# Four joints of the MLP in an encoder block on one core: a norm's scale, a load queue, two products and the last piece of tokens moved

## The chip, the cores and the metric

The program runs on one core of a Trainium2 chip. The core has five engines with an in-order queue each: TensorE (PE in the profile, its weight loads are PEld), VectorE (DVE), ScalarE (ACT), GpSimd (POOL) and SyncE (SP). They meet through semaphores. PE multiplies into PSUM, DVE and ACT read PSUM and work on SBUF, POOL works on SBUF alone, and DMA transfers are issued from the queues of SP, ACT and POOL. The metric is the device time of one execution in microseconds.

## The reference

One encoder layer on 1024 tokens of width 1024, all in float32. What is touched here is the MLP behind the attention and the last norm:

```python
        x = x + merged @ w_out[l]

        h2 = _rmsnorm(x, norm2_w[l])
        x = x + jnp.square(jax.nn.relu(h2 @ w_ff1[l])) @ w_ff2[l]

    return _rmsnorm(x, final_norm_w)
```

`_rmsnorm` divides each token by the root of its mean square and multiplies by a weight for each channel. The hidden width is 4096.

## The kernel before

Everything stands with channels on the 128 partitions and tokens on the free axis. `Y` is the residual, eight tiles of 128 x 1024. A float32 operand is split into a high part, rounded by ACT to the matmul's input type (`split`, line 170, `operand`, `prep`), and a low part, the difference, made by DVE. A product is then three passes: high times high, high times low, low times high.

**A visit** (class `Visit`, lines 1076 to 1123) multiplies a 2 x 2 grid of blocks with seven products instead of eight, after Winograd. `load` fetches two raw weight tiles from SP's queue into three `wraw` slots (line 1090), `blocks` makes four sums of weights (1096 to 1099), `prep` splits one of the seven (1107, 1108), `product` runs 3 x g matmuls of 512 columns into one of three PSUM banks (1119). Products 1, 6, 7 and 4 follow each other in one bank, 5 and 3 in another; a bank must have been read before the next product is added to it. `run` keeps `prep` three products ahead.

**First stage**, visits f0 to f15 (g = 4, 84 matmuls each): the first matrix of the MLP. The operands `XT` come from `Y` without the norm's factor, which is a number for each token. That factor, `r2`, is made by `norm2` (line 1207): four matmuls with ones over the sums of squares `xsq`, then `rsqrt` (lines 187 to 192, eight ACT steps and four DVE steps). `each1` runs it ahead of the second product of f0. f0 runs its products in the order `EARLY` = 1, 5, 2, 3, 6, 7, 4, the other visits in `USUAL` = 1, 2, 6, 5, 7, 3, 4. `ff1_done` copies products 1, 6, 7 and 5 to SBUF (1248), adds, and calls `act` (1242, 1243), which takes relu times `r2` and squares it. The results and their sums go to `d_u` in DRAM, from SP's and ACT's queues.

**Second stage**: the second matrix. Units 12 and 13 of the hidden width go through it without Winograd (`plain(NP2)`, lines 1399 to 1424): four operand pairs are loaded from `d_u` on SP's queue (1404), weights by `wtile` (146, 148, 150), and for each of eight output tiles `mm3` runs 24 matmuls (157) whose sum is added to `Y` (1415). Between them two steps of `u_prep` for each product begin the units of the visits behind: a unit is three tiles of 128 x 1024 and one of 128 x 512, loaded from `d_u` on SP's queue (1322, 1330) and split (1323, 1324, 1331, 1332). Then visits y0 to y14 follow `PLAN`: y0 has one unit (21 matmuls), y1 two, y2 three, y3 to y11 four, y12 three, y13 two, y14 one. Visit y3 is the first that needs unit 3; from there each visit to y11 needs a unit more. `each2` frees old units, makes sure of the needed one and takes one step of `u_prep` with each product. `ff2_done` adds each product to `Y` (1349). All big tiles come from one pool of `NUNIT` = 35 slots (`mem`).

**Last stage**: units 14 and 15 are multiplied plainly, in four pieces of 256 tokens (`PIECES`, lines 1460 to 1483). For each piece and each of eight output tiles, 12 matmuls (1470), a sum into `Y` (1472), a square (1474, 1477) and a sum of the squares on POOL or DVE (1478). `finish` then runs one matmul with ones (1451), `rsqrt`, eight scalings (1456) and eight stores from SP's queue (1458); its parts are taken between the next piece's tiles, and for the last piece behind it.

The order of instructions on each engine is made by a list scheduler from the source's order, the data and the free slots; the source's order is a priority.

The three places that set the joints:

```python
        if v.name == "f0" and i == v.order[1] and not state1[0]:
            state1[0] = True
            norm2()
...
                nc.sync.dma_start(b.ap[:, sl], d_u[j0 + f // 2, q, :, RT if q or f % 2 else LT])
            split(a, b, b.ap)
...
    rest = iter(())
    for t0, t1 in PIECES:
```

## Time and profile before

| | us |
|---|---|
| median of three runs | 1676.75 |
| the three runs | 1674.54 to 1679.56 |
| the profiled execution, its own time | 1680.28 |
| its span in the profile | 1678.6 |

| engine | busy us | share of the span |
|---|---|---|
| PE | 1609.9 | 96% |
| PEld | 1329.0 | 79% |
| DVE | 1206.8 | 72% |
| ACT | 806.4 | 48% |
| POOL | 222.8 | 13% |

The MLP with the last norm takes the span from about 1016 us to its end. A busy share is a mean over the stretch it is taken from; matmuls overlap in the pipeline, so that a row's busy time for PE is best checked against the count of matmuls times the distance from one to the next. A timeline row merges neighbouring instructions of one kind: its second number is the whole stretch, and in square brackets stand the idle time before it and what ended it. "Issue" rows of SP are the moments at which transfers are sent off, not their landing.

### The profile page before, as it was taken

What the parts mean: (1) busy time and instruction counts of PE and PEld (TensorE: products, weight loads), DVE (VectorE), ACT (ScalarE), POOL (GpSimd) and SP (SyncE); (2) the same over time, 40 slices, a digit from 0 to 9 for tenths busy, and PEclk for the clock granted to TensorE, in tenths of its full rate; (3) what the DMA queues carried; (4) which work ended last, traced back from release to release, by engine and by line L of the source; (5) the groups of instructions that cost most, each with busy time, mean ns of one, the idle gap of its engine ahead of it and who ended that gap; (6) DMA issues with size and microseconds to landing.
All of it is one profiled execution on the core that took longest, in us unless ns stands there. A gap on an engine that the chain in (4) does not pass through costs nothing.

```text
span 1678.6 us, 21771 instructions
## 1 busy us (share of the span) xinstructions
PE 1609.9 (96%) x8201; PEld 1329.0 (79%) x8201; DVE 1206.8 (72%) x1751; ACT 806.4 (48%) x1365; POOL 222.8 (13%) x247
## 2 busy tenths in 40 slices
PE   8899999999989889999999998999999998999997
PEld 3687788877768877888878886888888777888886
DVE  5987999931335668888887668767776478788766
ACT  5567431441335558878762345444444443444333
POOL 1212100000003446545300000000000000000012
PEclk9999999999989999999999999999999999999998
DMA  4135243472234252111074211444343543444213
GB/s 180 62 108 132 80 163 113 139 213 88 76 101 132 57 163 89 39 39 39 26 250 138 89 50 56 164 149 152 138 165 118 190 167 113 163 163 145 82 57 101
DMA packets 85657, 196.87 MB, mean 117 GB/s; under 512 B 20128, under 2 KB 35744, under 8 KB 85296
## 3 DMA queue, kind: packets, MB, share of 16 engines
q1 hardware_dynamic: 61376, 153.95, 27.4%
q10 hardware_dynamic: 23360, 38.02, 6.5%
q0 software_dynamic: 816, 3.51, 1.0%
q8 instruction: 65, 1.06, 0.3%
q14 instruction: 40, 0.33, 0.1%
HBM read 135.22 MB, written 60.23 MB: 116 GB/s over the span
## 4 chain that ended last, share of the span: by engine, by line
PE 77%; DVE 9%; DMA 6%; ACT 4%; POOL 2%; issue 2%; ACTq 0%; SPq 0%; DVEq 0%; POOLq 0%
PE ps_z L157 15%; PE ps_af L1119 10%; PE ps_ay L1119 8%; PE ps_w L157 5%; PE ps_cf L1119 5%; PE ps_p L157 5%; PE ps_s L849 5%; PE ps_cy L1119 4%; PE ps_pv L891 4%; PE ps_pt L872 3%; PE ps_df L1119 2%; PE ps_y L157 2%; DMA f<-d_vl 2%; PE ps_y L1470 2%; PE ps_dy L1119 2%
## 5 line engine op out<-in xcount | busy, mean ns | idle before, releaser
L157 PE MATMUL ps_z<-u,wi_h 128*128 128x512 f32 x1088 | 258.0, 392 | 11.8 <-POOL u L171 2.9
L157 PEld LDWEIGHTS ps_z<-u,wi_h 128*128 128x128 f32 x1088 | 202.2, 188 | 58.7 <-ACT u L170 4.5
L1119 PE MATMUL ps_af<-u,f_w 128*128 128x512 f32 x768 | 182.4, 390 | 4.3 <-ACT u L1248 4.3
L1119 PEld LDWEIGHTS ps_af<-u,f_w 128*128 128x128 f32 x768 | 144.1, 188 | 34.9 <-ACT u L1248 5.1
L1119 PE MATMUL ps_ay<-u,y_w 128*128 128x512 f32 x576 | 140.5, 393 | 2.4 <-ACT y_w L1107 1.2
L157 PE MATMUL ps_z<-u,wi_l 128*128 128x512 f32 x544 | 136.2, 401 | 0.0
L1119 PEld LDWEIGHTS ps_ay<-u,y_w 128*128 128x128 f32 x576 | 108.3, 189 | 27.1 <-ACT y_w L1107 2.4
L1478 POOL TENSOR_TENSOR u<-u,q 128x256 f32<-128x256 f32 x20 | 15.3, 767 | 822.2 <-ACT q L1477 821.9
L157 PEld LDWEIGHTS ps_z<-u,wi_l 128*128 128x128 f32 x544 | 104.4, 194 | 22.2
L849 PE MATMUL ps_s<-u,u 128*128 128x512 f32 x384 | 104.9, 406 | 2.0 <-POOL u L838 1.4
L150 DVE TENSOR_TENSOR wi_l<-wi_r,wi_h 128x1024 fp32r<-128x1024 f32 x34 | 41.5, 1220 | 77.0 <-PE ps_z L157 61.5
L1119 PE MATMUL ps_cf<-u,f_w 128*128 128x512 f32 x384 | 95.3, 398 | 0.0
L852 DVE TENSOR_REDUCE sx<-ps_s 128x1 f32<-128x1024 f32 x64 | 77.9, 1218 | 19.5 <-PE ps_s L849 17.5
L854 ACT ACTIVATE u<-ps_s,sx 128x1024 f32<-128x1024 f32 x64 | 72.3, 1130 | 31.8 <-DVE sx L852 31.4
L1119 PEld LDWEIGHTS ps_cf<-u,f_w 128*128 128x128 f32 x384 | 73.6, 192 | 16.3 <-issue 0.5
L878 DVE TENSOR_TENSOR u<-ps_pt,u 128x512 fp32r<-128x512 f32 x128 | 82.2, 679 | 5.1 <-ACT u L877 5.1
L148 ACT CAST wi_h<-wi_r 128x1024 fp32r<-128x1024 f32 x34 | 35.7, 1050 | 104.0 <-PE ps_z L157 95.6
L856 POOL TENSOR_SCALAR u<-u,sx 128x1024 f32<-128x1024 f32 x64 | 72.4, 1135 | 84.7 <-DVE sx L855 81.9
L849 PEld LDWEIGHTS ps_s<-u,u 128*128 128x128 f32 x384 | 67.5, 189 | 14.1 <-POOL u L838 2.2
L1108 DVE TENSOR_TENSOR f_w<-f_r,f_w 128x512 fp32r<-128x512 f32 x48 | 33.1, 690 | 58.4 <-ACT f_w L1107 58.4
L1243 ACT ACTIVATE u<-u 128x512 f32<-128x512 f32 x64 | 40.5, 633 | 71.1 <-DVE u L1242 70.2
L1119 PE MATMUL ps_cy<-u,y_w 128*128 128x512 f32 x288 | 71.3, 391 | 2.5 <-DVE y_w L1108 2.1
(376 smaller groups left out, 3307.3 us busy)
## 6 DMA issues: line engine op xcount, KB each, us to landing
u<-d_u SPq DMA_DIRECT2D x36, 512.0 KB, 3.6
wi_r<-w_in SPq DMA_DIRECT2D x34, 512.0 KB, 3.5
f_r<-w_ff SPq DMA_DIRECT2D x32, 512.0 KB, 3.2
d_u<-u SPq DMA_DIRECT2D x24, 512.0 KB, 4.0
d_z<-f ACTq DMA_DIRECT2D x20, 512.0 KB, 3.2
f<-d_z SPq DMA_DIRECT2D x20, 512.0 KB, 4.2
y_r<-w_ff SPq DMA_DIRECT2D x18, 512.0 KB, 3.8
d_u<-u ACTq DMA_DIRECT2D x16, 512.0 KB, 2.6
```

The source lines that it names most:

```text
L148: A.copy(hi, raw)
L150: V.tensor_tensor(lo, raw, hi.bitcast(F32), ALU.subtract)
L157: T.matmul(ps[:, sl], w, x[:, sl], start=start, stop=stop)
L849: T.matmul(pss[:, sl], a.r[:, qsl], b.r[:, sl], start=i == 0, stop=i == 2)
L852: V.tensor_reduce(sx[:, 0:1], pss, AX.X, ALU.max, negate=True)
L854: A.activation(P.ap, pss, AF.Exp, bias=sx[:, 0:1], accum_out=sx[:, 1:2])
L856: G.tensor_scalar(P.ap, P.ap, sx[:, 1:2], 1.0, ALU.mult, ALU.mult)
L872: T.transpose(pt[:, k * 128:(k + 1) * 128], P.ap[:, ko:ko + 128], ident)
L878: V.tensor_tensor(lv, p3, hf_, ALU.subtract)
L891: T.matmul(pso[:, 0:256], VC[kb].r[:, h * 128:(h + 1) * 128], PT[kg][i].r[:, k * 256:(k + 1) * 256], start=kb == 0 and i == 0, stop=kb == ...
L1119: T.matmul(ps, w[:, a, k * 128:(k + 1) * 128], self.xops[k][i].parts[b], start=n == 0 and i in FIRST, stop=n == 3 * self.g - 1, skip_group ...
L1243: A.activation(t, t, AF.Square)
```

## The change

- `norm2` is called ahead of the fifth product of f0 (product 6) instead of the second. Until it has been called, `act` keeps its work on a list (`waiting`), and the list is worked off right behind it; only product 2's block is on it by then.
- The loads of `u_prep` and of `plain` are issued from POOL's queue (`G`) instead of SP's.
- The plain products are a generator. Six of eight run ahead of the visits; the seventh is put ahead of y0's second product, the eighth ahead of y1's second. The last weight tile is loaded and split ahead of the visits, into a pair of `mem`, and the operands are freed behind the eighth product. `each2` starts a new unit only if seven slots of `mem` are free.
- The pieces are 320, 320, 256 and 128 tokens. For the last one, the squares of the eight tiles stand in one tile and are summed by eight matmuls with ones into one PSUM bank; the norm's weight is multiplied in ahead; the factor is made in 128-column steps, and two multiplications of 512 columns are stored with two transfers, one from SP's queue and one from ACT's.

```diff
@@ -43,7 +43,7 @@
 
 
 ORDER = "kkkmrvGGklGtvSvvGsciiSigiigcSSgiQigQQiiQgQgQigQgiQqgigoggiKVKVViKgigogigzzqggzqKqzggV"
-PIECES = tuple((i, i + 256) for i in range(0, S, 256))
+PIECES = ((0, 320), (320, 640), (640, 896), (896, 1024))
 K0 = 6
 LEAD, LAG = 3, 2
 VS, VS2 = (3, 4), (0, 1)
@@ -1231,16 +1231,21 @@
 
     d_u = dr.tile([NP1, 4, 128, 1024], F32, name="d_u")
 
+    scaled, waiting = [], []
+
+    def act(t, src, half_):
+        if not scaled:
+            waiting.append((t, src, half_))
+            return
+        V.scalar_tensor_tensor(t, src, 0.0, r2.ap[:, half_], ALU.max, ALU.mult)
+        A.activation(t, t, AF.Square)
+
     def ff1_done(j):
         sa, sb = mem.alloc(), mem.alloc()
         uu = [mem.alloc() for _ in range(4)]
         s = {1: sa.ap[:, LT], 6: sa.ap[:, RT], 7: sb.ap[:, LT], 5: sb.ap[:, RT]}
         (b11, b21), (t2, t1), (t3, b22), (t4, b12) = [(u.ap[:, LT], u.ap[:, RT]) for u in uu]
         seen, bank = set(), []
-
-        def act(t, src, half_):
-            V.scalar_tensor_tensor(t, src, 0.0, r2.ap[:, half_], ALU.max, ALU.mult)
-            A.activation(t, t, AF.Square)
 
         def done(i, ps):
             seen.add(i)
@@ -1278,12 +1283,12 @@
                 t.free()
         return done
 
-    state1 = [False]
-
     def each1(v, i):
-        if v.name == "f0" and i == v.order[1] and not state1[0]:
-            state1[0] = True
+        if v.name == "f0" and i == v.order[4]:
             norm2()
+            scaled.append(True)
+            for w in waiting:
+                act(*w)
 
     class Lazy:
         def __init__(self, make):
@@ -1319,7 +1324,7 @@
             if len(ii) == 2:
                 hi, lo = mem.alloc(True), mem.alloc(True)
                 units[j] += [hi, lo]
-                nc.sync.dma_start(lo.ap, d_u[j, q])
+                G.dma_start(lo.ap, d_u[j, q])
                 A.copy(hi.r, lo.ap)
                 V.tensor_tensor(lo.r, lo.ap, hi.ap, ALU.subtract)
                 for i, sl in zip(ii, HS):
@@ -1327,7 +1332,7 @@
             else:
                 t = mem.alloc(True)
                 units[j].append(t)
-                nc.sync.dma_start(t.ap[:, RT], d_u[j, q, :, LT])
+                G.dma_start(t.ap[:, RT], d_u[j, q, :, LT])
                 A.copy(t.r[:, LT], t.ap[:, RT])
                 V.tensor_tensor(t.r[:, RT], t.ap[:, RT], t.ap[:, LT], ALU.subtract)
                 UT[j][ii[0]] = Half(t.r[:, LT], t.r[:, RT])
@@ -1389,7 +1394,9 @@
                     for t in units[j]:
                         t.free()
             need(PLAN[q][0])
-        if not preps and nextj[0] < NP2 and nextj[0] - len(freed) < LIVE:
+        if q in (0, 1) and i == v.order[1]:
+            next(pp)
+        if not preps and nextj[0] < NP2 and nextj[0] - len(freed) < LIVE and mem.live + 7 <= NUNIT:
             preps.append(u_prep(nextj[0]))
             nextj[0] += 1
         if preps and next(preps[0], preps) is preps:
@@ -1401,27 +1408,38 @@
         for f in range(4):
             a, b = mem.pair()
             for q, sl in zip(((0, 3), (0, 2))[f % 2], HS):
-                nc.sync.dma_start(b.ap[:, sl], d_u[j0 + f // 2, q, :, RT if q or f % 2 else LT])
+                G.dma_start(b.ap[:, sl], d_u[j0 + f // 2, q, :, RT if q or f % 2 else LT])
             split(a, b, b.ap)
             ul.append((a, b))
         return ul
 
-    ul = plain(NP2)
-    for mp in range(4):
-        w = wtile(w_ff2t[0, mp], f"w2_{mp}")
-        for m in (2 * mp, 2 * mp + 1):
-            ps = pa(f"ps_y{m}")
-            mm3(ps, w, m % 2 * 4, ul)
-            V.tensor_tensor(Y[m], ps, Y[m], ALU.add)
-            for _ in range(2):
-                if not preps and nextj[0] < 3:
-                    preps.append(u_prep(nextj[0]))
-                    nextj[0] += 1
-                if preps and next(preps[0], preps) is preps:
-                    preps.pop()
-    for a, b in ul:
-        a.free()
-        b.free()
+    def plain_products():
+        ul = plain(NP2)
+        for mp in range(4):
+            if mp < 3:
+                w = wtile(w_ff2t[0, mp], f"w2_{mp}")
+            for m in (2 * mp, 2 * mp + 1):
+                ps = pa(f"ps_y{m}")
+                mm3(ps, w if mp < 3 else [x.r for x in w3], m % 2 * 4, ul)
+                V.tensor_tensor(Y[m], ps, Y[m], ALU.add)
+                if m == 7:
+                    for t in w3 + [x for p in ul for x in p]:
+                        t.free()
+                yield
+
+    pp = plain_products()
+    for m in range(6):
+        next(pp)
+        for _ in range(2):
+            if not preps and nextj[0] < 3:
+                preps.append(u_prep(nextj[0]))
+                nextj[0] += 1
+            if preps and next(preps[0], preps) is preps:
+                preps.pop()
+    raw = wp.tile([128, 1024], F32, tag="wraw", name="w2_3r", bufs=3)
+    nc.sync.dma_start(raw, w_ff2t[0, 3])
+    w3 = list(mem.pair())
+    split(*w3, raw)
 
     vs = []
     for q, (_, m, j0, j1) in enumerate(PLAN):
@@ -1457,19 +1475,21 @@
                                    ALU.mult, ALU.mult)
             nc.sync.dma_start(out[m * 128:(m + 1) * 128, sl], Y[m][:, sl])
 
+    def piece(sl, n, m):
+        wh, wl = w2[m // 2]
+        ps = pb(f"ps_y{m}_{sl.start}")
+        for j, (w, i) in enumerate(((wh, 0), (wh, 1), (wl, 0))):
+            for k in range(4):
+                o = ((m % 2) * 4 + k) * 128
+                T.matmul(ps[:, 0:n], w[:, o:o + 128], ul[k][i].r[:, sl], start=j + k == 0,
+                         stop=j == 2 and k == 3)
+        V.tensor_tensor(Y[m][:, sl], ps[:, 0:n], Y[m][:, sl], ALU.add)
+
     rest = iter(())
-    for t0, t1 in PIECES:
+    for t0, t1 in PIECES[:-1]:
         sl, n = slice(t0, t1), t1 - t0
         for m in range(8):
-            wh, wl = w2[m // 2]
-            ps = pb(f"ps_y{m}_{t0}")
-            for j, (w, i) in enumerate(((wh, 0), (wh, 1), (wl, 0))):
-                for k in range(4):
-                    o = ((m % 2) * 4 + k) * 128
-                    x = ul[k][i].r
-                    T.matmul(ps[:, 0:n], w[:, o:o + 128], x[:, sl], start=j + k == 0,
-                             stop=j == 2 and k == 3)
-            V.tensor_tensor(Y[m][:, sl], ps[:, 0:n], Y[m][:, sl], ALU.add)
+            piece(sl, n, m)
             if m == 0:
                 A.activation(xsq.ap[:, sl], Y[m][:, sl], AF.Square)
             else:
@@ -1479,9 +1499,39 @@
             if m > 1:
                 next(rest, None)
         rest = finish(sl, n)
+
+
+    t0, t1 = PIECES[-1]
+    sl, n = slice(t0, t1), t1 - t0
+    sq, yn, yo = (mem.alloc().ap.rearrange("p (m c) -> p m c", m=8) for _ in range(3))
+    psn = psA.tile([128, 512], F32, tag="A", name="ps_n4")
+
+    def square_sum(m):
+        T.matmul(psn[:, 0:n], ones, sq[:, m], start=m == 0, stop=m == 7)
+
+    for m in range(8):
+        piece(sl, n, m)
+        A.activation(sq[:, m], Y[m][:, sl], AF.Square)
+        A.activation(yn[:, m], Y[m][:, sl], AF.Copy, scale=pcol(NF + m))
+        if m > 0:
+            next(rest, None)
+        if m > 1:
+            square_sum(m - 2)
     for _ in rest:
         pass
-
+    square_sum(6)
+    square_sum(7)
+    r, a_, b_ = r3.ap[:, sl], half("m")[:, 0:n], half("t")[:, 0:n]
+    V.tensor_scalar(a_, psn[:, 0:n], 1.0 / D, eps_t[:, 0:1], ALU.mult, ALU.add)
+    A.activation(r, psn[:, 0:n], AF.Ln, bias=eps_t[:, 0:1], scale=1.0 / D)
+    A.activation(r, r, AF.Exp, scale=-0.5)
+    A.activation(b_, r, AF.Square)
+    V.scalar_tensor_tensor(b_, b_, -0.5, a_, ALU.mult, ALU.mult)
+    V.scalar_tensor_tensor(r, b_, 1.5, r, ALU.add, ALU.mult)
+    for m0, eng in ((0, nc.sync), (4, A)):
+        ms = slice(m0, m0 + 4)
+        V.tensor_tensor(yo[:, ms], yn[:, ms], bcm(r, 4), ALU.mult)
+        eng.dma_start(out.rearrange("(m p) s -> p m s", p=128)[:, ms, sl], yo[:, ms])
```

## Rows read from the trace of the kernel before

**Rows 1.** Stretch, length, busy PE PEld DVE ACT POOL (count), clock, DMA share, GB/s.

```profile
1015.60:1047.00 31.40, 27.14 (x103) 20.49 (x102) 27.00 (x43) 19.79 (x35) 0.00 (x0) 0.89 0.10 33
1047.00:1329.90 282.90, 282.90 (x1249) 233.94 (x1247) 193.79 (x306) 128.63 (x223) 0.00 (x0) 1.00 0.40 146
1329.90:1342.80 12.90, 8.72 (x30) 6.10 (x29) 6.92 (x7) 5.24 (x6) 0.00 (x0) 0.87 1.00 351
1342.80:1380.30 37.50, 37.50 (x165) 31.07 (x166) 26.74 (x32) 14.98 (x20) 0.00 (x0) 1.00 0.51 187
1380.30:1398.40 18.10, 13.26 (x45) 8.55 (x43) 16.99 (x29) 8.78 (x18) 0.00 (x0) 0.91 0.39 130
1398.40:1417.00 18.60, 18.57 (x82) 15.30 (x83) 17.04 (x31) 5.46 (x10) 0.00 (x0) 1.00 0.30 102
1417.00:1604.00 187.00, 187.00 (x826) 154.84 (x825) 145.62 (x217) 71.78 (x103) 0.00 (x0) 1.00 0.39 128
...
1614.90:1665.00 50.10, 49.88 (x400) 48.88 (x399) 35.69 (x76) 19.70 (x46) 15.11 (x20) 1.00 0.21 70
1665.00:1678.60 13.60, 1.23 (x3) 0.50 (x2) 6.11 (x15) 2.50 (x6) 0.23 (x1) 0.59 0.41 135
```

**Rows 2.** Chain that ended last: start us, us, engine, tile, line, count.

```profile
1316.34 2.72 PE ps_af L1119 x12
...
1645.89 11.50 PE ps_y L1470 x96
...
1657.40 0.45 PE ps_n L1451 x2
```

**Rows 3.** Instructions in order of time, joint 1: start, us, engine, line, operation.

```profile
1018.80 1.97 PE L1210 MATMUL ps_n<-f,ones 128*128 128x512 f32 x4
...
1020.61 0.67 ACT L187 ACTIVATE f<-ps_n,eps_t 128x512 f32<-128x512 f32 x1
...
1028.75 0.68 ACT L190 ACTIVATE m<-ps_n,eps_t 128x512 f32<-128x512 f32 x1
...
1029.83 0.59 ACT L1248 COPY u<-ps_af 128x512 f32<-128x512 f32 x1
...
1030.47 0.79 PE L1119 MATMUL ps_af<-u,f_w 128*128 128x512 f32 x1 [4.25 <-ACT u L1248]
...
1031.06 5.18 PE L1119 MATMUL ps_cf<-u,f_w 128*128 128x512 f32 x12
```

**Rows 4.** Waits of SP's queue, 1290 to 1345: us in total, times, longest.

```profile
SPq L146 <- DVE w_l L150: 4.5, 1, 4.5
```

**Rows 5.** Order of time, joint 2.

```profile
1326.34 1.75 SPq L1404 DMA_DIRECT2D u<-d_u  x4
...
1333.13 4.47 PE L157 MATMUL ps_y<-u,w_h 128*128 128x512 f32 x12 [3.19 <-ACT u L170]
```

**Rows 6.** Groups from 1380.3 to 1417: count | busy us, mean ns | idle before.

```profile
L1324 DVE TENSOR_TENSOR u<-u,u 128x1024 fp32r<-128x1024 f32 x5 | 6.1, 1219 | 1.1 <-ACT u L1323 1.1
...
L1107 ACT CAST y_w<-s 128x128 fp32r<-128x128 f32 x3 | 0.9, 300 | 1.3 <-PE ps_y L157 0.5 <-PE ps_ay L1119 0.4 <-PE ps_dy L1119 0.4
L1108 DVE TENSOR_TENSOR y_w<-s,y_w 128x128 fp32r<-128x128 f32 x3 | 0.8, 280 | 0.0
```

**Rows 7.** DMA issues: queue, count, KB each, median us to landing.

```profile
u<-d_u SPq DMA_DIRECT2D x36, 512.0 KB, 3.6
...
SY<-d_g POOLq DMA_DIRECT2D x2, 1024.0 KB, 10.1
```

**Rows 8.** Chain again, the tail.

```profile
1666.24 0.35 DVE f L1472
...
1667.60 1.24 PE ps_n L1451 x2
...
1673.28 1.58 DVE f L1456 x4
```

**Rows 9.** Line 467, one source line.

```profile
DMA to landing us min/median/max: 7.7/10.1/12.5
```

## The prediction

> **What bounds the kernel now.** I read the table of stretches first [rows 1], then the chain of work that ended last [rows 2], then each joint's order in time. In the long middles TensorE (PE) is never late: from 1047 to 1329.9 us, and again from 1417 to 1604, its busy time equals the stretch and the granted clock is 1.00. There a 512-column matmul costs 2.72/12 = 0.227 us, and a 256-column one 11.50/96 = 0.120 [rows 2]. So only the joints hold anything, and what each loses is its length less its matmuls at these prices.
>
> Joint 1, from 1015.6 to the end of the first MLP stage at 1329.9: 16 visits x 84 matmuls x 0.227 = 304.7, and 1.97 for the four norm matmuls [rows 3]. The first matmul starts at about 1015.9, so 314.1 are used and 7.4 lost. Joint 2 with the plain products, 1329.9 to 1380.3: 192 x 0.227 = 43.5 of 50.4, lost 6.9. Joint 3, visits y0 to y2, 1380.3 to 1417.0: 126 x 0.227 = 28.6 of 36.7, lost 8.1. All of that falls before 1398.4: 45 matmuls are worth 10.2 of 18.1 there, and 82 fill the next 18.6 [rows 1]. Joint 4, 1417 to 1665: 882 x 0.227 + 384 x 0.120 + three norms of 0.45 = 247.3 of 248, lost 0.7. Joint 5 is the tail behind PE's last product, 1665.0 to 1678.6: 13.6. Together 36.7 us are open.
>
> **The change part by part.**
>
> **Joint 1, scale later.** After product 1, PE runs norm2's four matmuls. ScalarE's (ACT's) in-order queue then takes norm2's eight steps between the casts for the last operands, the first at 1020.61 and the last at 1028.75. The two copies of line 1248, which free the banks for products 3 and 6, come only behind them, from 1029.83 on. PE stands idle for 4.25 us until they end, and the next 12 matmuls take some 5 us instead of 2.72 [rows 3]; the stretch's granted clock is 0.89 [rows 1]. Idle, slow matmuls and small change make the 7.4. The change moves norm2 three products later. From 1020.61 to the copy at 1029.83 ACT takes 17 instructions, 0.54 each, so the copies move up by about eight x 0.54 = 4.3 us, the whole idle, and with it goes the slow clock. What comes late next: the norm matmuls today cover the time in which the casts of XT[3] are made (1.97 less the 0.54 that these move up: 1.4), and after the move the eight steps stand before the copies of s[6] and s[7], which the last three products of f0 need one after the other on one bank. f1's first product also needs a bank that norm2's results hold. I charge 1.3 for the second and 1.4 for the first: 2.7 stay, 4.7 are gained. The bounds are 0, if the wait only moves, and 6.9. VectorE's (DVE's) one held-back scaling waits for r2; behind it stand other evictions of f0, which is part of the 1.3.
>
> **Joint 2, loads from POOL's queue.** SP's queue is in order. The second weight load of line 146 waits 4.5 us for a slot that a subtraction at line 150 frees [rows 4]. Behind it stand the eight loads of line 1404, the first four issued only at 1326.34, 3.6 us before PE is out of work, and PE's first plain matmul waits until 1333.13 for a cast of them [rows 5]. DMA share is 1.00 in that stretch [rows 1]: all comes at once. On POOL's queue the loads wait for their own slots alone. XT[..][1] and XT[..][2] are last read by the first two products of visit f15, so eight slots are free five products of 2.72 = 13.6 us before its end. POOL has nothing else to do: its busy time is 0.00 from 1015 to 1604 [rows 1]. Four casts on ACT and four subtractions of 1.22 on DVE [rows 6] then fall beside f15's last products; DVE is busy 194 of 283 us in that stage [rows 1]. I take 6.0 of the 6.9. The lower bound is 1, if the loads come as late as now and only the queue of issues is gone; the upper is 6.9.
>
> The Trainium skill, DMA: Bandwidth & Descriptors, section Issuing engines are not separate DMA queues, says that issuing from several engines only saves the issuing sequencer's time, since all run on the same 16 engines. By that rule joint 2 would give about 1 us instead of 6, a rival below. The rows on SP's waits speak against it here: what is saved is not issue time but a wait for someone else's slot in front.
>
> **Joint 3, two plain products in the first visits.** y0 and y1 have 1 and 2 blocks, so a product lasts 0.7 or 1.4 us, less than its cast, subtraction and eviction. DVE is busy 17.0 of 18.1 us [rows 1]. The two moved products are 48 x 0.227 = 10.9 us of PE work, with little DVE work (one sum of 1.2 us each). They leave the plain stage, so the visits begin 10.9 earlier, and fill a stretch that has 7.9 us of idle PE. Against it: six products instead of eight carry fewer steps of u_prep; unit 2 ends in y0, and the guard on free units keeps unit 3 waiting until the plain operands are freed in y1. Each unit is three subtractions of 1.22 [rows 6] and one of 0.68 = 4.3 us of DVE. From the plain stage to y3 DVE does 26.7 + 17.0 + 17.0 = 60.7 us [rows 1]; if the stretch shrinks from 74 to 68, that is 89%, and it is late-heavy. I let 3.1 of the 8.1 stay: 5.0 gained, bounds 1.5 (DVE bound throughout) and 7.5. Unit 3 is needed at y3, some 22 us after its slots come free, so its loads fit. The extra pair for the last weights is the same cast and subtraction, only earlier: nothing.
>
> **Joint 4** has nothing to give: 0, bounds -1 and +0.7. Behind POOL's last eight loads stand its additions of line 1478, which start only after them in data order anyway.
>
> **Joint 5, the tail.** The columns stay 1024, so the pieces cost the same by the line through 0.227 and 0.120 (0.066 at 128 columns). The 128-column price has no row; ends 0.066 and 0.120, I take 0.08, nearer the line: 96 x 0.014 = +1.3. Six sums of squares on PE ahead of the tail are worth 0.22 to 0.25 each: +1.4. PE so ends at about 1667.7. One more us for the last sum behind the third piece's eight scalings on DVE (now too it starts 1.2 behind PE, at 1666.24 [rows 8]): 1668.7. Then the chain, with 128-wide steps at 0.28 to 0.30 [rows 6] plus 0.06 between engines: addition and square 0.7, last sum 0.7 (1.24 now for 256 columns), three ACT steps 1.2, two DVE steps 0.7, two multiplications of 512 columns 1.4 = 4.7. Now the last scaling ends at 1674.86 [rows 8] and the span 3.7 us later; two stores of 256 KB on two queues instead of four waiting on one, some 3.0. The end is 1676.4: 2.2 gained. The bounds are 0 (128-column matmuls no cheaper than 256-column ones) and 5.
>
> **Sum**: 4.7 + 6.0 + 5.0 + 0 + 2.2 = 17.9. The profiled execution took 1680.28 for a span of 1678.6, so 1662.4 for it; it lies 3.5 above the median of the three runs, 1676.75. Against that median: 1658.9, say 1659.
>
> **The rivals.**
>
> *The queue buys nothing* (the rule above). If the loads wait for slots rather than for SP's order, joint 2 gives 1 and joint 3 half: 4.7 + 1 + 2.5 + 2.2 = 10.4, 1666. For it: SP's loads in the long stage do wait for slots. Against: the 4.5 us of [rows 4] directly ahead of the late loads.
>
> *The norm's wait comes back* (also the case that the change doesn't do what it says). The order on each engine is planned by data that is ready, not by the source alone: the norm matmuls may go into the same hole as now, or the copies of s[6] may wait as those of s[1] do. Joint 1 gives 0: 13.2, 1663.5.
>
> *Slower: POOL's loads land late.* Each visit of 84 matmuls is 19.0 us, and in it one unit's four loads must land, with 2.3 for the last cast and subtraction: the point is 4.2 us a load. SP's take 3.6, and POOL has only two large ones, of 1024 KB, issued together [rows 7]; the later took 12.5 [rows 9]. If loads of 512 KB took half of that later one each, 6.25, one after the other, a unit needs 25 + 2.3 = 27.3, and eight visits (y4 to y11) wait 8.2 each: +66 - 18, 1725. Against it: 2 MB in 12.5 us is 164 GB/s, so 512 KB in 3.2, and loads overlap.
>
> The Trainium skill, SBUF — State Buffer, section SBUF: two separate sides, adds that POOL's descriptors wait while VectorE runs a two-port mode, as a copy does. By that rule each load could wait for one DVE step, and joint 2 would lose 1 to 2 us; but DVE's steps in these stretches are two-source ones [rows 6], and no run here shows such a wait.
>
> *Every joint closes*: 6.9 + 6.9 + 7.5 + 5 = 26, 1650.
>
> **How the numbers follow.** Forecast 0.60, queue rival 0.14, norm rival 0.11, slower rival 0.06, all closed 0.09. A difference under 0.3% (5 us) can't be told from none. The queue rival's 10 us lie near that with its low ends: I put 0.05 of it, and 0.01 of the norm rival, at no change. Faster 0.60 + 0.09 + 0.10 + 0.09 = 0.88, same 0.06, slower 0.06. The range runs from 1650 (all closed) to 1669, where the queue rival has 3 us more to lose; beyond lie the slower case, the same and a few hundredths below.
>
> **What would show it.** Joint 1: copies of line 1248 ahead of the norm's ACT steps, and no PE gap over 2 us before f1. Joint 2: loads issued from POOL before 1320, and a plain matmul straight behind f15. Joint 3: PE idle in y0 and y1 under 4 us, DVE over 90%. Tail: some 11 us behind PE's last 128-column product. PE waits ahead of first products of y4 to y11 would show the slower case. Wrong would be the forecast if one of these waits stands again under another name.

## The result and the profile after

The changed kernel takes 1685.36 us (median of five runs, 1682.39 to 1689.15); the kernel before took 1677.23 beside it. The ratio is 1.0059, with a 95% interval of 1.0045 to 1.0073: slower by 0.6%, where 1659 had been forecast and 1650 to 1669 given as the range. The profiled execution after took 1685.28 us with a span of 1683.6, 5.0 more than the profiled one before.

The first step is to cut both spans at the same six points, so that every joint has a number. The points are read from PE's timeline: f0's first matmul, the end of f15, y3's first matmul (inside a merged row, by 0.227 us from one matmul to the next), y13's second product (its first row of `ps_dy`), the end of the last matmul of a piece, and the end of the span.

| stretch, us | before | after | difference | forecast |
|---|---|---|---|---|
| f0's first matmul to f15's end (joint 1) | 314.08 | 313.24 | -0.8 | -4.7 |
| f15's end to y3 (joints 2 and 3) | 87.03 | 86.88 | -0.2 | -11.0 |
| y3 to y13 (the long middle) | 187.05 | 189.75 | +2.7 | 0 |
| y13 to the end of the last piece | 61.00 | 68.47 | +7.5 | +3.7 |
| behind it | 13.59 | 8.43 | -5.2 | -5.9 |

With 1.0 of drift ahead of f0, where nothing was changed, these make the 5.0. The table of stretches of the changed kernel, which answers [rows 1] (stretch and length, busy PE, PEld, DVE, ACT, POOL with counts, clock, DMA share, GB/s):

```profile
1016.80:1047.00 30.20, 26.29 (x101) 20.11 (x100) 26.95 (x42) 20.27 (x35) 0.00 (x0) 0.89 0.10 35
...
1330.10:1341.60 11.50, 4.62 (x12) 3.31 (x12) 4.50 (x6) 5.35 (x6) 1.71 (x4) 0.76 1.03 410
1341.60:1373.90 32.30, 32.27 (x132) 26.51 (x133) 20.36 (x24) 8.69 (x12) 0.00 (x0) 0.93 0.09 31
1373.90:1398.00 24.10, 23.40 (x101) 18.44 (x100) 22.79 (x37) 12.05 (x21) 3.21 (x6) 1.00 0.48 153
1398.00:1417.00 19.00, 17.54 (x77) 13.90 (x76) 19.00 (x32) 7.37 (x12) 0.00 (x0) 1.00 0.35 112
1417.00:1606.70 189.70, 187.52 (x826) 154.68 (x825) 145.98 (x218) 69.96 (x103) 19.22 (x36) 1.00 0.37 127
...
1664.70:1675.10 10.40, 9.64 (x85) 9.46 (x84) 5.14 (x16) 5.42 (x18) 0.00 (x0) 1.00 0.32 102
```

Two lines speak at once. In the first one the clock is 0.89, as before: joint 1's hole is still there. And from 1330.1 to 1341.6 PE works 4.6 of 11.5 us while the DMA engines are full (share 1.03, 410 GB/s); in the next stretch they are nearly empty (0.09). Something was fetched too early and all at once.

**Joint 1** in the timeline after (start, us, engine, line, operation; in brackets the idle time before and what ended it), beside [rows 3]:

```profile
1020.92 1.88 PE L1210 MATMUL ps_n<-f,ones 128*128 128x512 f32 x4
...
1024.52 0.67 ACT L187 ACTIVATE f<-ps_n,eps_t 128x512 f32<-128x512 f32 x1
...
1028.24 0.63 ACT L188 ACTIVATE f<-f 128x512 f32<-128x512 f32 x1
...
1029.66 0.62 ACT L1136 CAST u<-t 128x512 fp32r<-128x512 f32 x1 [0.79 <-DVE t L1166]
...
1030.19 0.58 ACT L1253 COPY u<-ps_af 128x512 f32<-128x512 f32 x1
...
1030.82 0.79 PE L1119 MATMUL ps_af<-u,f_w 128*128 128x512 f32 x1 [3.91 <-ACT u L1253]
...
1031.41 4.98 PE L1119 MATMUL ps_cf<-u,f_w 128*128 128x512 f32 x12
```

The norm's matmuls stand in the old hole although the source calls them three products later, and four of its eight ACT steps (line 187 and 188, twice each) still run ahead of the copies. Counted from f0's first matmul the copy starts after 13.36 us, before after 13.98. It now stands behind a cast (line 1136) that itself waits 0.79 us for DVE. The hole is 3.91 us instead of 4.25, and the slow 12 matmuls are still 4.98.

**Joint 2** in the timeline after, beside [rows 5]:

```profile
1313.19 4.37 POOL L1411 DMA_DIRECT2D u<-d_u  x8 [484.46 <-DMA d_u<-u]
...
1330.83 0.63 ACT L1241 ACTIVATE u<-u 128x512 f32<-128x512 f32 x1 [1.36 <-DVE u L1240]
1330.93 0.54 POOL L1327 DMA_DIRECT2D u<-d_u  x1 [0.18 <-issue]
1331.37 1.03 ACT L170 CAST u<-u 128x1024 fp32r<-128x1024 f32 x1
...
1331.96 0.38 SPq L1090 DMA_DIRECT2D y_r<-w_ff  x1
...
1332.30 2.93 ACT L170 CAST u<-u 128x1024 fp32r<-128x1024 f32 x3
...
1332.45 4.62 PE L157 MATMUL ps_y<-u,w_h 128*128 128x512 f32 x12 [2.38 <-ACT u L170]
...
1340.15 0.29 DVE L1096 TENSOR_TENSOR s<-y_r 128x128 f32<-128x128 f32 x1 [6.50 <-DMA y_r<-w_ff]
1340.36 3.49 DVE L171 TENSOR_TENSOR u<-u,u 128x1024 fp32r<-128x1024 f32 x3
...
1341.63 1.65 PE L157 MATMUL ps_y<-u,w_h 128*128 128x512 f32 x3 [4.56 <-DVE u L171]
```

POOL sends the eight loads off at 1313, 13 us earlier than SP did, just as forecast. It is of little use, because the first cast (line 170) keeps its place on ACT behind the last step of f15 (line 1241). And POOL doesn't stop: behind these eight it has sent off thirteen unit loads (lines 1327 and 1335) by 1331.5. SP's load of `y_r`, 128 KB for y0, comes at 1331.96 into full DMA engines:

```profile
DMA to landing us min/median/max: 8.2/8.2/8.2
```

(one source line, 1090, in this stretch). Before, the same load took 5.2:

```profile
DMA to landing us min/median/max: 5.2/5.2/5.2
```

DVE's next instruction in order is line 1096, which needs `y_r`. It waits 6.50 us, and the three subtractions of line 171 that PE needs stand behind it, though the casts that they need are done by 1335.2. Over the whole execution, the units' loads of 512 KB take longer on POOL's queue than the 3.6 us of SP's [rows 7] (DMA issues after: queue, count, KB each, median us to landing):

```profile
u<-d_u POOLq DMA_DIRECT2D x36, 512.0 KB, 4.3
```

### The profile page after: what moved, and what is told of

It reads as the page before. It is cut to its first block, busy times and chain, and to the rows that moved or that the text cites. A ratio compares the mean times of both kernels' runs of the same rounds, so it can differ in the third digit from the quotient of the medians.

```text
span 1683.6 us, 21810 instructions
## 1 busy us (share of the span) xinstructions
PE 1616.2 (96%) x8215; PEld 1337.2 (79%) x8215; DVE 1206.4 (72%) x1744; ACT 806.7 (48%) x1372; POOL 256.0 (15%) x306
## 4 chain that ended last, share of the span: by engine, by line
PE 77%; DVE 8%; DMA 6%; ACT 4%; issue 3%; POOL 1%; SPq 0%; ACTq 0%; DVEq 0%; POOLq 0%
PE ps_z L157 17%; PE ps_af L1119 10%; PE ps_ay L1119 6%; PE ps_w L157 5%; PE ps_p L157 5%; PE ps_cf L1119 5%; PE ps_s L849 5%; PE ps_pv L891 3%; PE ps_cy L1119 3%; PE ps_pt L872 3%; PE ps_y L157 3%; PE ps_df L1119 2%; PE ps_y L1484 2%; DMA u<-d_u 2%; DMA f<-d_vl 2%
## 5 line engine op out<-in xcount | busy, mean ns | idle before, releaser
L1411 POOL DMA_DIRECT2D u<-d_u x16 | 8.6, 549 | 500.8 <-DMA d_u<-u 484.5
```

## The experiments

All but e12 are timed in five rounds against the kernel before on the same chip (median 1676.5 to 1676.9). The table gives the ratio with its interval, and the five stretches of the profiled execution. The first two rows repeat the result.

| run | ratio, 95% interval | f0 to f15's end | to y3 | to y13 | to the last piece's end | behind |
|---|---|---|---|---|---|---|
| before | 1 | 314.08 | 87.03 | 187.05 | 61.00 | 13.59 |
| after | 1.0059 (1.0045 to 1.0073) | 313.24 | 86.88 | 189.75 | 68.47 | 8.43 |
| e1_norm | 0.9997 (0.9985 to 1.0009) | 312.84 | 85.59 | 187.36 | 60.70 | 13.46 |
| e2_pool | 1.0041 (1.0028 to 1.0055) | 314.30 | 89.67 | 189.18 | 60.89 | 13.13 |
| e3_visits | 0.9993 (0.9981 to 1.0006) | 314.07 | 84.85 | 187.03 | 60.85 | 13.12 |
| e4_tail | 1.0051 (1.0036 to 1.0066) | 313.46 | 86.80 | 186.99 | 69.93 | 8.71 |
| e5_order | 0.9979 (0.9964 to 0.9995) | 308.46 | 86.48 | 187.60 | 60.60 | 13.47 |
| e6_plain | 0.9988 (0.9974 to 1.0002) | 314.14 | 83.06 | 187.89 | 60.89 | 13.87 |
| e7_units | 1.0049 (1.0034 to 1.0065) | 314.02 | 95.74 | 187.00 | 60.59 | 13.13 |
| e8_t256 | 1.0007 (0.9990 to 1.0023) | 314.42 | 86.48 | 187.00 | 62.57 | 11.39 |
| e9_three | 0.9943 (0.9927 to 0.9959) | 308.36 | 80.77 | 187.56 | 60.97 | 13.49 |
| e10_t384 | 0.9936 (0.9924 to 0.9948) | 308.37 | 80.85 | 187.38 | 62.26 | 11.31 |
| e11_sp_units | 1.0026 (1.0015 to 1.0037) | 313.88 | 80.99 | 187.95 | 75.58 | 8.74 |
| e12_tail_again | a single time, 1686.31 us | 313.45 | 86.98 | 187.00 | 74.52 | 8.73 |

Where a run leaves a stretch alone, it repeats within 1.0 us of the others (the one to y3 within 1.5), so the stretches can tell more than the totals, which spread by several us from run to run. The first four runs do one part of the change each.

### e1_norm: the scale later, alone

The edit is the hunks on `act`, `waiting` and `each1` of the change, and no other.

> The kernel before with the first part alone: the norm's scale taken three products later. Theory (after the trace of the changed kernel): the planner puts the norm's matmuls and ACT steps back into the same hole, so only 0.8 us are gained: ratio 0.9995, and PE again waits some 4 us for a copy of ACT ahead of the last products of f0. Rival (the forecast's term): 4.7 us gained, ratio 0.9972, and no PE gap over 2 us there.

Measured: 0.9997, and joint 1 is 1.2 us shorter, hardly more than the 1.0 by which that stretch repeats. The gap ahead of the copy's reader is 3.91 us again, ended by line 1253. The theory holds; the forecast's 4.7 don't come.

### e5_order: the copies planned ahead of the norm

```diff
+    def behind(ins):
+        for c in first:
+            tc.add_manual_dep(ins.ins, c.ins.name, nosync, reason="order")
...
-            A.copy(t.r[:, LT], src)
+            behind(A.copy(t.r[:, LT], src))
...
-        before = ln_exp_table(after) if after is not None else lambda ins: None
+        before = ln_exp_table(after) if after is not None else order
...
+        if v.name == "f0" and i == v.order[2]:
+            for _ in xo3:
+                pass
...
-                A.copy(s[i], ps)
+                ins = A.copy(s[i], ps)
+                if len(first) < 2:
+                    first.append(ins)
```

(`xo3` is the rest of `x_odd(3)`, the operands of products 7 and 4; `order` is `behind` for the norm's first step of each half. The dependency is for the plan alone and sets no semaphore.)

> The first part alone, and beside it an order laid down for the plan: the last three casts of operand XT[3] wait for nothing new, but the casts for products 7 and 4 and all eight ACT steps of the norm are planned behind the first two copies of f0. Theory: the copies' place in ACT's in-order queue is the cause of PE's gap; it falls from 3.9 us to under 1, the 12 matmuls behind it take 2.7 to 3 us instead of 4.6, f0's first matmul to f1's third product takes 25 us instead of 30: ratio 0.997. Rival: another wait takes its place (the operands for products 7 and 4, or r2): ratio 0.999 or above.

Its timeline, to be held against the one of joint 1 above:

```profile
1025.69 0.58 ACT L1259 COPY u<-ps_af 128x512 f32<-128x512 f32 x1
1026.17 0.59 ACT L1259 COPY u<-ps_cf 128x512 f32<-128x512 f32 x1
...
1026.33 0.96 PE L1119 MATMUL ps_af<-u,f_w 128*128 128x512 f32 x3 [0.84 <-ACT u L1259]
1027.12 2.91 PE L1119 MATMUL ps_cf<-u,f_w 128*128 128x512 f32 x12
```

The copy starts 10.30 us after f0's first matmul (1015.39) instead of 13.98, the gap is 0.84, and the 12 matmuls behind it take 2.91 instead of 5.18: the granted clock is 1.00 throughout. From f0's first matmul to f1's second product in its order (the first row of `ps_df` behind f0, which the theory calls the third) go 25.4 us, as the theory had it, against 31.0 before. The stretch is 5.6 us shorter than before, and the ratio 0.9979. Here is all that joint 1 promised, and the cause of its hole is shown: the copies' place in ACT's queue, not the call's place in the source. The edit takes two things from in front of the copies, the norm's steps and the casts for products 7 and 4; no run parts them.

### e2_pool, e6_plain, e7_units: which loads do the harm

Each puts loads from `d_u` on POOL's queue: e6 those of `plain`, e7 those of `u_prep`, e2 both.

```diff
-                nc.sync.dma_start(b.ap[:, sl], d_u[j0 + f // 2, q, :, RT if q or f % 2 else LT])
+                G.dma_start(b.ap[:, sl], d_u[j0 + f // 2, q, :, RT if q or f % 2 else LT])
...
-                nc.sync.dma_start(lo.ap, d_u[j, q])
+                G.dma_start(lo.ap, d_u[j, q])
...
```

> The kernel before with the second part alone: all loads from d_u (those of the plain operands and those of the units) issued by POOL. Theory: POOL puts more transfers on the DMA engines at once, SP's 128 KB load of y_r lands late, DVE's queue stands behind it, and one late unit load stalls DVE in the long middle: 4 us lost at the plain products, 2.7 more in the middle, together +6 to +7, ratio 1.004. Rival one (the forecast's term): 6.0 gained, ratio 0.9964. Rival two (the loads' order doesn't matter, the loss of the changed kernel came with its other parts): ratio within 0.001 of 1.

> The kernel before with only the eight loads of the plain operands on POOL's queue; the units' loads stay on SP's. Theory: the harm of the second part came from the units' loads, which nothing paces on POOL; without them y_r lands in some 4 us, PE's waits at the plain products are one of 2.4 us (ACT's first cast behind f15's last step), and joint 2 loses 3.5 to 4.5 instead of 6.9: ratio 0.998. Rival: early plain loads are of no use since the casts keep their place on ACT and DVE, ratio 0.9995 to 1.0005; or they do harm themselves: 1.002.

> The kernel before with only the units' loads on POOL's queue; the plain operands' stay on SP's. Theory: the units' loads fill the DMA engines ahead of the plain operands and of y_r; joint 2 loses 4 us or more over before, and the long middle 2 to 3 more: ratio 1.0035 to 1.005. Rival: only both together do harm: ratio within 0.001 of 1.

Together (e2) they lose: 1.0041, 2.6 us up to y3 and 2.1 in the middle. The plain loads alone (e6) gain 4.0 us up to y3 in the profile; the interval of the timed ratio, 0.9974 to 1.0002, holds these 4.0 and also none. The units' loads alone (e7) lose 8.7 there. PE's waits at the plain products, in e6:

```profile
1327.18 0.38 SPq L1090 DMA_DIRECT2D y_r<-w_ff  x1
...
1327.67 7.55 PE L157 MATMUL ps_y<-u,w_h 128*128 128x512 f32 x25 [2.38 <-ACT u L170]
...
1330.09 0.30 DVE L1096 TENSOR_TENSOR s<-y_r 128x128 f32<-128x128 f32 x1 [1.22 <-DMA y_r<-w_ff]
1330.30 3.49 DVE L171 TENSOR_TENSOR u<-u,u 128x1024 fp32r<-128x1024 f32 x3
```

and in e7:

```profile
1333.74 1.04 ACT L170 CAST u<-u 128x1024 fp32r<-128x1024 f32 x1 [6.31 <-DMA u<-d_u]
...
1334.84 5.20 PE L157 MATMUL ps_y<-u,w_h 128*128 128x512 f32 x12 [8.80 <-ACT u L170]
...
1341.53 0.29 DVE L1096 TENSOR_TENSOR s<-y_r 128x128 f32<-128x128 f32 x1 [5.48 <-DMA y_r<-w_ff]
```

In e6 SP sends `y_r` off ahead of the units' loads, it lands in 2.9 us, and DVE loses 1.22. What is left at the plain products is the wait of 2.38 and the low clock behind it (0.54 from 1328 to 1330; 25 matmuls in 7.55 us that are worth 5.7). In e7 fourteen unit loads have been sent by 1327.5; the first plain loads, which PE needs first, go off at 1322.4 behind eight of them, and `y_r` at 1328.7 behind all:

```profile
DMA to landing us min/median/max: 8.8/10.7/13.7
...
DMA to landing us min/median/max: 12.8/12.8/12.8
```

(lines 1404, eight plain loads, and 1090, `y_r`, of e7). So five runs give `y_r` 2.9 us without POOL's unit loads (e6), 5.2 before, 8.2 after and in e2, 12.8 in e7: the harm is the units' loads, which SP's order had held back behind the weights and the plain operands, and which on POOL wait for nothing but a free slot.

The Trainium skill, DMA: Bandwidth & Descriptors, section Issuing engines are not separate DMA queues, says that transfers from all issuing engines run on the same 16 engines and interleave, and that a second issuer only saves the sequencer's time. The first half is what e7 shows, at 8.7 us; the second half misses what decided here, since the queue also set the order in which the transfers were let go. By that rule joint 2 would have gained about 1 us. In e6 the plain products lose 4.0 us instead of 6.6, which is 2.6.

The 2.1 us in the middle of e2, and most of the 2.7 after, are one or two late transfers in front of an in-order engine. The chain of waits after:

```profile
1527.34 6.48 DMA u<-d_u
...
1533.84 1.06 ACT u L1328
...
1534.92 1.23 DVE u L1329
...
1537.48 0.61 DVE f L1354
...
1538.22 2.98 PE ps_ay L1119 x12
```

PE waits 1.4 us there for DVE's line 1354, which stands behind a unit's subtraction. Another 0.7 are lost at 1569, in a visit where DVE waits 2.1 us for a `y_r`; e11, whose units come from SP, has that wait too (0.7). In e2 it is a `y_r` that DVE waits 4.3 us for, and PE 1.6; in e7 PE doesn't wait in the middle at all, though its units come from POOL too. Why these loads are late in two of three such kernels stays open.

### e3_visits: two plain products in the first visits, alone

The edit is the hunks on `plain_products`, `pp` and the guard with `mem.live`, with all loads on SP's queue.

> The kernel before with the third part alone: two plain products moved into y0 and y1, all loads still on SP's queue. Theory: PE loses 3.7 us instead of 8.1 in y0 to y2, so 4.4 gained, ratio 0.9974. Rival: with SP's in-order queue the units' loads come late for y3 and give the gain back, ratio 0.999 to 1.001.

Measured: 0.9993, and 2.2 us less up to y3, half of the theory's 4.4. The rival is nearer. The engines' busy time in two stretches of e3 (columns as in the first table):

```profile
1369.00:1391.90 22.90, 21.83 (x95) 17.25 (x94) 20.10 (x34) 10.60 (x20) 0.00 (x0) 1.00 0.54 184
1391.90:1406.90 15.00, 12.73 (x51) 10.13 (x52) 15.00 (x25) 5.97 (x10) 0.00 (x0) 0.91 0.37 122
```

and what PE does in the second one:

```profile
1404.52 3.82 PE L1119 MATMUL ps_ay<-u,y_w 128*128 128x512 f32 x9 [2.27 <-DVE f L1349]
```

DVE is busy 15.00 of 15.00 us, some 6 of them with subtractions for units that came late; PE waits 2.27 for an eviction behind them, and then runs 9 matmuls in 3.66 us instead of 2.04. In e9 below, where the plain loads come early, the same wait of 2.25 us stays in y2, but the 9 matmuls behind it take 2.34 in their row and not 3.82. From y0 to y3 PE loses 6.2 us in e3, where the first unit load goes off 5.4 us behind f15's end, 4.6 in e9 and e11 (2.4 behind it), and 3.6 after (12.5 ahead of it). By these runs this part gives more where the units' loads are sent earlier.

### e4_tail, e12_tail_again, e8_t256: the tail alone

e4 and e12 are the kernel before with the change's `PIECES`, `piece` and new end. e8 changes one size in it:

```diff
-PIECES = ((0, 320), (320, 640), (640, 896), (896, 1024))
+PIECES = tuple((i, i + 256) for i in range(0, S, 256))
...
-    sq, yn, yo = (mem.alloc().ap.rearrange("p (m c) -> p m c", m=8) for _ in range(3))
+    sq, yn, yo = ([mem.alloc().ap.rearrange("p (m c) -> p m c", m=4) for _ in range(2)]
+                  for _ in range(3))
```

> The kernel before with the last part alone: pieces of 320, 320, 256 and 128 columns and the last piece's own end. Theory: a 128-column matmul takes 0.108 us, so 96 of them cost 4.0 us over the line, the sums of squares and two waits 3.4 more, the chain behind PE is 5.1 shorter: 2.3 us lost, ratio 1.0014. Rival (the forecast's term): 2.2 gained, ratio 0.9987. Either way PE's last product should end about 10 us later than before and the span 8.5 us after it.

> A second look at the last part alone (pieces of 320, 320, 256, 128). Theory: TensorE's clock is not always kept in the last piece: in the first look the last 18 matmuls ran at the low level (12 in 2.6 us instead of 1.3). If the whole piece runs so, it costs 8 x 1.3 = 10.4 us and the time comes to some 1689; if none of it does, some 1677. Rival: the piece always runs at 0.108 a matmul and the times differ for other reasons.

> The last part alone with one size changed: four pieces of 256 columns as before, the last with the new end (its squares, scaled rows and products in two tiles each). Theory: the loss of the last part is the price of 128-column matmuls, and their clock; with 256 columns they cost 0.120 us again, the eight sums of squares add 1.9, the chain behind PE's last product is 9 to 10 us instead of 13.6: ratio 0.9985, and the times spread no more than those of before. Rival: the new end itself loses (its sums on PE and waits): ratio 1.001 or above, and the spread stays.

The last piece in the timeline after, at full clock all through. PE has run two of its eight products before the sum of the third piece (line 1469), which a merged row ahead of these lines hides:

```profile
1664.39 0.70 PE L1469 MATMUL ps_n<-u,ones 128*128 128x256 f32 x2 [1.00 <-DVE u L1498]
...
1667.97 1.54 PE L1484 MATMUL ps_y<-u,u 128*128 128x128 f32 x12
1669.34 0.43 PE L1510 MATMUL ps_n<-u,ones 128*128 128x128 f32 x2
1669.53 1.54 PE L1484 MATMUL ps_y<-u,u 128*128 128x128 f32 x12
1671.83 0.49 PE L1510 MATMUL ps_n<-u,ones 128*128 128x128 f32 x2 [0.76 <-ACT u L1514]
```

From one product's start to the next (1667.97 to 1669.53) go 1.56 us. The chain of waits splits them into the product and its sum:

```profile
1672.32 1.29 PE ps_y L1484 x12
1673.61 0.27 PE ps_n L1510 x2
1673.88 1.30 PE ps_y L1484 x12
```

So 12 matmuls take 1.30, 0.108 each with 128 columns, where 256 columns take 0.120 [rows 2]. Half the columns cost 90%. Eight products so pay 96 x (0.108 - 0.066) = 4.0 over the line, the five sums ahead of the last product's end 5 x 0.27 = 1.35, and the two waits (1.00 and 0.76) 1.76: 7.1 of the 7.5 measured. Why the price hardly falls is not shown. The weight loads (PEld, 128 x 128 whatever the matmul's columns) are busy 83% of the long stretch with 512 columns, 98% with 256 [rows 1], and in the last piece for 9.46 us where PE is busy for 9.64; that they set the floor would fit, and no run tests it.

e12 shows that this is the good case. Two stretches of its last pieces, and then, from its timeline, one product:

```profile
1650.00:1661.00 11.00, 9.99 (x85) 9.80 (x84) 8.39 (x19) 4.21 (x13) 2.52 (x3) 1.00 0.35 119
1661.00:1676.00 15.00, 15.00 (x73) 15.00 (x72) 5.38 (x16) 3.92 (x13) 0.00 (x0) 0.50 0.22 72
```

```profile
1661.12 2.80 PE L1466 MATMUL ps_y<-u,u 128*128 128x128 f32 x12
```

From the fourth product of the 128-column piece on the granted clock is 0.50, the low one of the two levels (1.2 GHz), and it stays there though PE is busy 15.00 of 15.00 us; a product and its sum take 2.99 us (1661.12 to 1664.11) instead of 1.56, and the piece ends 4.6 us later than in e4 by its stretch (74.52 to 69.93). In e4 the clock is low only for the last product and the sums behind it; in e11 from the piece's third product on; after, nowhere in the piece. PE waits 1.0 us behind the piece's second product in all four, so what decides it these runs don't show. e12's 1686.31 us lie between the theory's 1677 and 1689; the rival, one price throughout, is refuted.

The mean granted clock that is listed for each timed run bears this out, though it doesn't say where the clock was low. It is under 0.980 in 6 of e4's 12 runs, 6 of e11's 12 and 2 of the changed kernel's 5, all with the 128-column piece, in one each of e7 and e8, and in none of the 78 runs of the kernel before that were timed beside the experiments. e4's six take 1682.8 to 1691.0 us, its other six 1676.6 to 1684.5. So e4's timed ratio, 1.0051, is above both its theory (1.0014) and its rival: by the profile it loses 8.9 up to the last piece's end, 1.5 of them by the clock, and gains 4.9 behind.

e8, with 256 columns, keeps the clock in its profile: from product to product go 1.85 us all through the piece. Its times spread over 12.4 us, those of the kernel before beside it over 13.2. With the sums, the piece's end comes 1.6 later than before; the chain behind it is 2.2 shorter. That leaves 0.6, and the timed ratio, 1.0007, doesn't show it. The theory was right on the price and too hopeful on the gain: behind the last product the new end still has 11.4 us, of which two multiplications of 1024 columns take 2.36.

The Trainium skill, TensorE: Matmul & The Clock Gate, section Back-to-back issue gap, gives about 81 ns for each 128-column matmul in a stream with weight loads. Worked out as an estimate, the piece would cost 96 x 0.027 = 2.6 us less by that page. The trace does not agree: it has 0.108, and that decides.

### e11_sp_units: one edit of the changed kernel undone

```diff
-                G.dma_start(lo.ap, d_u[j, q])
+                nc.sync.dma_start(lo.ap, d_u[j, q])
...
-                G.dma_start(t.ap[:, RT], d_u[j, q, :, LT])
+                nc.sync.dma_start(t.ap[:, RT], d_u[j, q, :, LT])
```

> The changed kernel with one edit undone: the units' loads go back to SP's queue, the plain operands' stay on POOL's. Theory: joint 2 falls by 4 us or more and the middle's late load (2.7) is gone, so 6 to 8 us less than the changed kernel: ratio to the kernel before 0.999 to 1.002. Rival: the changed kernel's loss has another cause, ratio 1.005 to 1.006.

The stretch to y3 falls from 86.88 to 80.99 us, the middle from 189.75 to 187.95, `y_r` lands in 3.0 us. That is 7.7 in all, as the theory has it. The timed ratio, 1.0026, is 0.0033 below the changed kernel's, some 5.5 us, and just above the theory's 0.999 to 1.002 (interval 1.0015 to 1.0037). The profiled execution ran its last piece at the low clock (75.58 for that stretch, 7.1 more than after), which hides the gain in its total.

### e9_three and e10_t384: what the parts give without their faults

e9 is e5's edit, e6's and e3's on the kernel before, with the old tail. e10 adds e8's end with three pieces:

```diff
-PIECES = tuple((i, i + 256) for i in range(0, S, 256))
+PIECES = ((0, 384), (384, 768), (768, 1024))
```

> Three edits on the kernel before: the norm's steps planned behind f0's first two copies, only the plain operands' loads on POOL's queue, two plain products in y0 and y1; tail as before. Theory: the joints add up, 5.6 + 4.0 + 2.2 = 11.8 us less, ratio 0.993; if the units' loads, freed of the eight loads ahead of them on SP's queue, come earlier, 2 more. Rival: joints 2 and 3 share DVE, whose subtractions only move from one to the other: 5.6 + 2 at most, ratio 0.9955.

> The same three edits, and the new end with three pieces of 384, 384 and 256 columns instead of four of 256. Theory: the new end with 256 columns gave 0.6 us in its profile; one piece less saves 96 matmuls' fixed part, 96 x 0.013 = 1.2; together 1.8 less than the run with three edits, ratio to the kernel before 0.992. Rival: the 384-wide scalings and squares make the last piece wait, and nothing is gained: the same as with three edits.

e9 takes 1666.96 us, ratio 0.9943. Its stretches are 5.7 shorter in joint 1 and 6.3 up to y3; together 12.0, as the 11.8 that were added up from the single runs, and against the rival joints 2 and 3 keep both gains (2.6 and 3.6). The timed medians are 9.9 apart, and the interval, 0.9927 to 0.9959, holds the theory's 0.993 and the rival's 0.9955; it is the stretches that decide. While the plain products run, PE is busy throughout, into y1 (the first stretch of the table after 1330 in e9):

```profile
1330.00:1366.00 36.00, 36.00 (x160) 29.60 (x159) 24.15 (x31) 13.09 (x18) 0.00 (x0) 1.00 0.40 148
```

e10 takes 1665.87, ratio 0.9936, with an interval that overlaps e9's: of the theory's 1.8 us the profile has 0.9 (62.26 + 11.31 against 60.97 + 13.49), and they lie inside the measurement. Both beat the kernel before and the changed one.

## Why the prediction was wrong, step by step

**What bounds the kernel**: right. The joints are where time can be had, and 36.7 us were open; e9 took 12 of them by its profile (9.9 by the timed medians), with three of the four ideas.

**Joint 1** (4.7 forecast, 0.8 measured, within the 1.0 by which the stretch repeats): the step that failed is "the copies move up by about eight x 0.54". They moved up by 0.6. It took the order of the source for the order of ACT's queue: four of the eight steps stayed in front, and with the other four gone ACT waited 0.79 us for DVE at the last cast ahead of the copies. The rival that the norm's wait comes back named just this, the matmuls going into the same hole; it had 0.11. The size was right once the order was made: e5 has 5.6, within the bound of 6.9.

**Joint 2** (6.0 gained forecast; lost time up to y0 rose from 6.6 to 11.1, by 43.83 us for 144 matmuls at 0.227): two steps failed. First, the loads did come early, and landed in 3.7 to 5.8 us, but the casts were held to "fall beside f15's last products", and their place on ACT and DVE is not made by their data. That left a wait of 2.38 us in every kernel with early plain loads (after, e2, e6, e9, e11). Second, the change moves the units' loads as well, and the prediction priced them only in visits y4 to y11, not here, where they meet `y_r`. It had the row: DMA share 1.00 in that stretch [rows 1] with SP's order still pacing the loads. With the units' loads left on SP, joint 2 loses 4.0 to 4.2 (e6, e11), so some 2.5 of the 6.0 were to be had.

**Joint 3** (5.0 forecast): y0 to y2 with two products take 43.05 us after for 174 x 0.227 = 39.5 of work, so 3.6 are lost instead of 8.3: 4.7 gained, right in size, but by luck in part: the early unit loads that harm joint 2 help here, and with them on SP's queue it is 3.6 (e9). Alone (e3) it is 2.1, near its lower bound of 1.5, and for the reason given for that bound: DVE is busy throughout the 15 us of y1 and y2 shown above. In the sum of the changed kernel the 4.5 that joint 2 loses hide the 4.7 that joint 3 gains.

**Joint 4** (0, bounds -1 and +0.7): 2.7 lost, outside the bounds. The slower rival had the mechanism, a unit load on POOL that lands late, with a wait in eight visits and 66 us; it came in one place, not eight: of the 2.7, PE waits 1.4 behind a late unit load and 0.7 behind a late `y_r`. The other 0.6 has no wait of its own in the profile, and is within what the stretch repeats to.

**Joint 5** (2.2 gained forecast, 2.3 lost): the chain behind PE was about right, 8.43 against 4.7 + 3.0 = 7.7. Mis-sized was the 128-column matmul, taken at 0.08, "nearer the line" between 0.066 and 0.120; it is 0.108, which makes 96 x 0.028 = 2.7 us. The waits in the piece are 1.8 where 1.0 was allowed; the sums were right (1.35 against 1.4). And the forecast had one clock for the piece, where e12 shows two; this costs nothing in the profiled execution after, and 6 to 7 us in e12 and e11.

**Sum**: 17.9 forecast to be gained, 5.0 lost by the profiles. The 22.9 between them are 3.9 (joint 1), 10.8 (joints 2 and 3), 2.7 (joint 4), 4.5 (joint 5) and the 1.0 of drift ahead of f0. The timed medians are 8.1 apart, because the profiled execution before lies 3.1 above its kernel's median and the one after at it. Of the changed kernel's five runs the two longest, 1687.58 and 1689.15, are also the two with the lowest granted clock, 0.977 and 0.978, as a last piece at the low clock would have it; their traces are not kept.

## What to carry to other kernels

Where a planner sets the order, a call moved in the source is no move: look at where the instruction stands in its engine's queue, and lay the order down if it matters. Before a group of loads goes to an idle queue, ask what the old queue's order held back, and which small load in front of an in-order engine will then land behind the group. A price between two sizes is not a price below the smaller one: measure narrow matmuls before cutting the last piece.

## What the runs showed of the hardware

- A 128-column float32r matmul of this stream takes 0.108 us at full clock; 256 columns take 0.120, 320 take 17.30/118 = 0.147 (from 1621.92 to 1639.22 after). The line through 256 and 512 ends somewhere above 128.
- The same stream of narrow matmuls kept the full clock in one execution (after) and lost it at three different points in three others (e4, e11, e12), with no PE wait over 1.01 us in the piece. Once low it stayed low to the end of the piece, with PE busy throughout (15.00 of 15.00 us in e12).
- A 128 KB load landed in 2.9 us when it was sent ahead of the units' loads (e6), and in 8.2 (after) and 12.8 us (e7) when 13 and 14 loads of 256 and 512 KB had been sent before it from another queue. In the first of these the DMA engines were full (share 1.03, 410 GB/s).
